# A hybrid mLSTM and short-conv block in fp32 on TensorE: post-processing cut into stages that take turns, and a first phase of two interleaved items

## The chip, the cores and the metric

One core of a Trainium2 chip runs the whole program. The metric is the time of one execution on the device in microseconds, as a median over runs. Below, PE is TensorE (its weight loads are PEld), DVE is VectorE, ACT is ScalarE, POOL is GpSimd and SP is SyncE, which here only issues DMAs.

## What is computed

One block over 512 tokens of width 2048, all in fp32:

```python
hn = rmsnorm(h, norm_mix_g)
proj = hn @ w_in + b_in
(q, k, v, o_pre, i_pre, f_pre, cb, cc, ch, gm_pre, gc_pre) = split(proj)
hm = mlstm_chunkwise(q, k, v, i_pre, f_pre)          # 4 heads, dqk 128, dv 256
hm = hm * rsqrt(mean(hm * hm) + EPS) * mlstm_head_g * sigmoid(o_pre)
y_m = hm @ w_branch_m
y_c = (cb * causal_dwconv(cc * ch, conv_w)) @ w_branch_c
h = h + (sigmoid(gm_pre) * y_m + sigmoid(gc_pre) * y_c) @ w_out
hn = rmsnorm(h, norm_ffn_g)
gate, val = split(causal_dwconv(hn @ w_up, ffn_conv_w, ffn_conv_b))   # 5504 each
h = h + (silu(gate) * val) @ w_down
return rmsnorm(h, norm_out_g)
```

## The kernel before

Each large product is done on TensorE in fp32r with operands split in two: a high part (`hi`, a copy on ACT that rounds) and a low part (`lo`, the difference, on DVE), and three matmuls, high by high, high by low, low by high. On top of that the 2 by 2 blocks of a product are formed in seven products instead of eight, which needs sums of weight blocks and of activation blocks. A **weight** (a raw tile, high halves `wh`, low halves `wl`) gets two of its sums by DMA: `fill` puts a block in place from SP's queue (L242, L243) and POOL issues DMAs that add another block to it (L245); DVE makes the other two (`s2` L210, `s4` L215). A **cell** (a pair of activation blocks) has its sums on DVE (`t3` L333, `e` L338, `t4` L343), its high part on ACT (L347), its low part on DVE (L350).

The program is a list of 476 steps (an item, a part q of its contraction), then 16 of another form. A step is 2 cells by 7 products by 3 matmuls of 128 by 256, 42 in all (L271, L272, L273), ahead of which PE waits for the weight's halves and for its banks. The phases in order are x (40 items of 4 steps: the input projection), yc and ym (the branches), out, up (the first feed-forward product), down, and a last part. An item's sums stand in half of bank 3 (`P_BANK`) and in one of two sets of three banks. When the item ends, ACT copies the first part to a z tile (`evac_first`, L295) and DVE makes the rest (`evac_ops`, L301 to L304) in the next step. At the ends of a phase two items are interleaved, their steps in turn.

The order on every engine is written by the loop: in step s DVE makes the two sums of weight s+2, the low parts of weight s+1 and of cells, ACT the high parts of weight s+2. There are six raw tiles, four `wh` and three `wl`, eight activation tiles. Loads are issued by SP, stores by ACT, a step after they are asked for (`late`).

What an item needs after its evacuation is its **post**, a list of pieces with a cost. Before, all pieces stand in one queue, and each step takes pieces from its front as long as a running credit allows. A piece may hold both ACT and DVE work: `normed` (L642, a multiplication by rstd on DVE, 1.22 us) and the activations on ACT behind it are one piece.

Next to it runs a **side** list: of each entry the PE part is issued at the end of a step, the post part at the start of the next one. It uses bank 7 (`SIDE`). The row sums, the gates and, from step 38, the four mLSTM heads go through it (24 entries a head): `b_pe` and `b_post` form the decayed scores, `v_pe` and `v_post` transpose v, `c_pe` and `c_post` form the output rows and their normalisation (L600 to L613), `t_pe` and `t_post` transpose back (L621, L627). Between two of them stands an empty entry, `gap`. `rsqrt_cols` (L399 to L411) is a scaling on DVE, a square root on ACT and five DVE operations.

At the start the first item runs alone, steps 0 to 3, one cell at a time as it comes: main matmuls, the gate matmuls of the cell (`gate_mm`, L471 to L476; i and f pre-activations), and the sum over its squares (`sum_tokens`, L420). The raw x of a cell goes through one of five buffers (mA, mB, z2, z0, z1), is scaled into a raw tile (L891, L892), and is squared in place after that (L899); cells 5 to 7 reuse the first three buffers, once their sums are done.

Of the kernel before, what the change touches and what calls it, by code (L numbers as in the profile page):

```python
# [69 lines left out]
def tile_block(ctx: ExitStack, tc: tile.TileContext, xT, w1, w_v0, w_v1, w_v2, w_bm, w_bc, w_out, w_up, w_down,  # L70
# [126 lines left out]
    def weight_task(it, q):  # L197
# [35 lines left out]
        t.load, t.sums, t.hi, t.lo = load, [s2, s4], hi, lo  # L233
        return t
# [20 lines left out]
    def rows_load(w, c0):  # L255
        def load(raw, q):
# [50 lines left out]
    def cell_task(xs, c, d, scale=None, key=None, eight=False):  # L307
# [14 lines left out]

        def diff():
# [3 lines left out]
        def t3():  # L327
            x = slots(t.raw)
            if scale:
                for ap, k in zip(two_k(), (k1, k2)):  # L330
                    A.activation(ap, ap, AF.Copy, scale=scale(k))
# [24 lines left out]
        t.two, m = two_k, 6 * SW if eight else NW  # L356
        t.cost = (0.65, 1.7) if eight else (1.35, 1.95)
# [3 lines left out]
    def direct_cell(xs, c, it, d=None, scale=None, key=None, eight=False):  # L361
# [11 lines left out]
        def t3():  # L373
            assert it.done
            a, b = t.two()
            if d is not None:
                V.tensor_add(a, a, it.z[:, :T])
                V.scalar_tensor_tensor(b, it.z[:, T:], -1.0, b, op0=ALU.mult, op1=ALU.subtract)
            else:
                A.activation(a, it.z[:, :T], AF.Copy, scale=scale(k1))  # L380
                A.activation(b, it.z[:, T:], AF.Copy, scale=scale(k2))
# [17 lines left out]
    def rsqrt_cols(dst, src, scale, eps, n):  # L399

        v, y, t = sm("nv")[:, :n], sm("ny")[:, :n], sm("nt")[:, :n]
# [21 lines left out]
    def rows_stages(ps, dst, diag, nt=4):  # L423

        def cols_post():
            rsqrt_cols(rs1[:, :nt], ps[:, :nt], 1.0 / D, EPS, nt)
# [33 lines left out]
    def gate_mm(c, x):  # L460
# [918 lines left out]
```

## Time and profile before

| what | value |
|---|---|
| median of 3 runs | 2686.89 us (2686.54 to 2688.54) |
| profiled execution, its own time | 2686.18 us |
| its span | 2684.5 us |
| busy, PE / DVE / ACT / POOL | 96% / 79% / 48% / 30% |
| granted PE clock, mean | 0.99 |

The span is the part of the execution in which the engines have instructions; the own time is measured around it, 1.7 us more. A row of the profile that reads "out<-in" names the tiles by their names in the program without their numbers, and "L273" is line 273 of the kernel. A wait is put down to the one that ended last.

### The profile page before, as it was taken

Reading aid. Unit: us, or ns where it says so; the run is one execution under the profiler, and the core shown is the slowest. Engines: PE = TensorE matmul, PEld = TensorE weight load, DVE = VectorE, ACT = ScalarE, POOL = GpSimd, SP = SyncE. Lnnn points to the kernel's source line nnn. Section 1 sums busy time; section 2 is a strip of 40 time slices with the busy share of each in tenths; the row PEclk is TensorE's granted clock in tenths of the full one; section 3 lists DMA queues with packets and bytes.
Section 4 is the critical chain, followed back from the end, with each engine's and each line's share of the span. In section 5 each row is a group of like instructions: output and inputs, shape, how many; then the busy total and the mean of one; then the engine's idle time right before and its main releaser. Section 6 shows DMA issues by size and latency. Waiting matters only on the chain.

```text
span 2684.5 us, 55468 instructions
## 1 busy us (share of the span) xinstructions
PE 2587.5 (96%) x21148; PEld 2564.8 (96%) x21148; DVE 2112.7 (79%) x3304; ACT 1278.2 (48%) x1735; POOL 801.6 (30%) x931
## 2 busy tenths in 40 slices
PE   7899999999999999999799999999999999999998
PEld 6899998999999999899799999999999989999997
DVE  5677777887777788977889988888888887676756
ACT  6444554445554443444545444444444554444433
POOL 3343333233333211121233333333333223232320
PEclk9899999999999999999999999999999999999999
DMA  7799989898989797797788888889888889798976
GB/s 193 177 230 235 246 228 229 215 243 223 253 228 233 205 297 221 212 252 207 204 223 219 223 222 225 221 222 228 218 222 227 206 216 226 188 226 207 238 173 200
DMA packets 464860, 594.64 MB, mean 222 GB/s; under 512 B 43040, under 2 KB 299040, under 8 KB 464592
## 3 DMA queue, kind: packets, MB, share of 16 engines
q1 hardware_dynamic: 303120, 420.84, 49.5%
q0 software_dynamic: 134240, 125.09, 31.6%
q10 hardware_dynamic: 27232, 45.17, 4.6%
q8 instruction: 165, 2.70, 0.4%
q14 instruction: 103, 0.84, 0.1%
HBM read 533.26 MB, written 57.67 MB: 220 GB/s over the span
## 4 chain that ended last, share of the span: by engine, by line
PE 52%; DVE 6%; DMA 4%; issue 2%; ACT 1%; POOL 0%; SPq 0%; DVEq 0%; POOLq 0%; ACTq 0%
PE bank L273 17%; PE bank L271 17%; PE bank L272 17%; DMA raw<-in_w_down_dram 2%; DVE wl L229 2%; DVE act L350 1%; DMA raw<-in_w_out_dram 1%; DMA raw<-in_w_up_dram 1%; DVE z L302 1%; DVE z L301 0%; PE bank L420 0%; PE bank L1095 0%; PE bank L1096 0%; DVE raw L210 0%; PE bank L1097 0%
## 5 line engine op out<-in xcount | busy, mean ns | idle before, releaser
L273 PE MATMUL bank<-act,wl 128*128 128x256 f32 x6760 | 1924.0, 285 | 39.3 <-DVE wl L229 35.9
L271 PE MATMUL bank<-act,wh 128*128 128x256 f32 x6760 | 1930.9, 286 | 14.7 <-DVE z L301 8.1
L272 PE MATMUL bank<-act,wh 128*128 128x256 f32 x6760 | 1919.7, 284 | 0.3 <-DVE act L350 0.3
L273 PEld LDWEIGHTS bank<-act,wl 128*128 128x128 f32 x6760 | 1304.2, 193 | 47.2 <-DVE wl L229 42.9
L271 PEld LDWEIGHTS bank<-act,wh 128*128 128x128 f32 x6760 | 1304.4, 193 | 19.3 <-DVE z L301 9.1
L272 PEld LDWEIGHTS bank<-act,wh 128*128 128x128 f32 x6760 | 1304.2, 193 | 3.6 <-issue 1.8
L225 ACT ACTIVATE wh<-raw 128x896 fp32r<-128x896 f32 x856 | 804.0, 951 | 1018.5 <-PE bank L272 682.0
L229 DVE TENSOR_TENSOR wl<-raw,wh 128x896 fp32r<-128x896 f32 x856 | 928.5, 1086 | 220.2 <-PE bank L273 149.6
L245 POOL DMA_DIRECT2D raw<-in_w_up_dram x344 | 299.1, 957 | 616.6 <-DMA raw<-in_w_up_dram 252.1
L245 POOL DMA_DIRECT2D raw<-in_w_dram x288 | 251.2, 950 | 551.2 <-DMA raw<-in_w_dram 274.3
L210 DVE TENSOR_TENSOR raw<-raw 128x256 f32<-128x256 f32 x428 | 179.2, 419 | 40.6 <-DMA raw<-in_w_down_dram 21.6
L245 POOL DMA_DIRECT2D raw<-in_w_down_dram x112 | 100.4, 1017 | 279.8 <-DMA raw<-in_w_down_dram 126.4
L215 DVE TENSOR_TENSOR raw<-raw 128x256 f32<-128x256 f32 x428 | 178.5, 417 | 0.2
L347 ACT ACTIVATE act<-xraw 128x1792 fp32r<-128x1792 f32 (+1 forms) x52 | 85.6, 1646 | 67.3 <-DVE xraw L343 56.6
L301 DVE TENSOR_TENSOR z<-bank,z 128x512 f32<-128x512 f32 x131 | 89.9, 686 | 28.4 <-ACT z L295 17.2
L183 ACT ACTIVATE wh<-raw 128x256 fp32r<-128x256 f32 x96 | 40.0, 416 | 130.1 <-PE bank L272 117.7
L350 DVE TENSOR_TENSOR act<-xraw,act 128x1792 fp32r<-128x1792 f32 (+1 forms) x52 | 101.7, 1956 | 0.0
L642 DVE TENSOR_TENSOR z<-z,rstd 128x1024 f32<-128x1024 f32 x83 | 101.0, 1218 | 0.0
L302 DVE TENSOR_TENSOR z<-bank,z 128x512 f32<-128x512 f32 x131 | 89.6, 684 | 1.8
L304 DVE TENSOR_TENSOR z<-bank,z 128x512 f32<-128x512 f32 x131 | 89.5, 683 | 0.0
L188 DVE TENSOR_TENSOR wl<-raw,wh 128x256 fp32r<-128x256 f32 x96 | 40.4, 421 | 57.9 <-PE bank L273 33.0
L245 POOL DMA_DIRECT2D raw<-in_w_out_dram x48 | 41.8, 972 | 129.6 <-DMA raw<-in_w_out_dram 64.0
(214 smaller groups left out, 1368.5 us busy)
## 6 DMA issues: line engine op xcount, KB each, us to landing
raw<-in_w_up_dram SPq DMA_DIRECT2D x172, 512.0 KB, 5.8
raw<-in_w_dram SPq DMA_DIRECT2D x144, 512.0 KB, 5.8
raw<-in_w_up_dram SPq DMA_DIRECT2D x344, 128.0 KB, 4.2
raw<-in_w_up_dram POOLq DMA_DIRECT2D x344, 128.0 KB, 5.1
raw<-in_w_down_dram SPq DMA_DIRECT2D x80, 512.0 KB, 5.2
raw<-in_w_dram SPq DMA_DIRECT2D x288, 128.0 KB, 4.1
raw<-in_w_dram POOLq DMA_DIRECT2D x288, 128.0 KB, 5.2
raw<-in_w_out_dram SPq DMA_DIRECT2D x32, 512.0 KB, 5.2
```

The costliest lines, as they stand in the source:

```text
L210: V.tensor_add(x[:, 6], x[:, 5], x[:, 0])
L215: V.tensor_add(x[:, 2], x[:, 6], x[:, 1])
L225: A.activation(seven(t.wh[r]), half(r), AF.Copy)
L229: V.tensor_sub(seven(t.wl[r]), half(r), seven(f(t.wh[r])))
L245: G.dma_start(at(i), a21, accum_op=ALU.add)
L271: PE.matmul(ps, h, xh, start=start, stop=False, skip_group_check=True)
L272: PE.matmul(ps, h, xl, start=False, stop=False, skip_group_check=True)
L273: PE.matmul(ps, l, xh, start=False, stop=stop, skip_group_check=True)
L301: return [lambda: V.tensor_add(z[:, 0:4:3], b0, two(z[:, 1])), lambda: V.tensor_add(z[:, 1:3], b1, two(z[:, 3])), lambda: V.tensor_add(z[: ...
L302: lambda: V.tensor_add(z[:, 1:3], b1, two(z[:, 3])),
L350: V.tensor_sub(t.act[:, NW:NW + m], t.raw[:, :m], f(t.act[:, :m]))
L642: V.tensor_mul(sb_pair(it.z), sb_pair(it.z), two(rstd))
```

## The change

- **Start.** The first two items are interleaved and START = 8 steps are done cell by cell in the order in which cells and weights come. Four weights (`ALONE`: items 0 and 1, q = 0, 1 and 2 of item 0) are loaded bare, without fills and adding DMAs; a new DVE operation `s13` makes those two sums. Cells 5 to 7 are loaded into their own raw tile and squared from there ahead of the scaling. The warm-up tile is cleared first on POOL, with 18 warm-up matmuls and not 20. The gate weights are made in step 8 in a raw slot (`held` takes it out of the loads' count), and `gate_mm` runs in steps 9, 10 and 11. The loads of the small parameters come after the start.
- **Posts.** Every item has its own list; up to two items give one piece each per step. `normed` is a piece of its own, the activations the next, and so for conv, out and up: pieces with DVE work and pieces with ACT work are apart. The order is conv: normed, Identity, product, taps; out: residual, square, sum; up: normed, Identity, taps of the first half, silu with taps of the second, product.
- **Side.** `rsqrt_cols` is cut in two, `rsqrt_a` up to the square root and `rsqrt_b` behind it; the second halves of `b_post` and `c_post` (`b_post2`, `c_post2`) stand in what was the empty entry, so that they run one step later.
- **Cells.** Where a cell is scaled on ACT, the scaling (`t.pre`) is issued a step ahead of its sums when its tile is there.

```diff
+ALONE = ((0, 0), (1, 0), (0, 1), (0, 2))
...
+        def s13():
+
+            x = slots(t.raw)
+            V.tensor_add(x[:, 4:6], x[:, 0:4:3], two(x[:, 2]))
...
         t.load, t.sums, t.hi, t.lo = load, [s2, s4], hi, lo
+        if (it.num, q) in ALONE:
+            t.sums = [s13, s2, s4]
...
-        def load(raw, q, eight=False):
-            if not eight:
+        def load(raw, q, bare=False):
+            if not bare:
                 fill(raw, [w[n, :, k0 + 4 * q + i:k0 + 4 * q + i + 2, :] for n in (n1, n2) for i in (0, 2)])
...
+        t.pre = scaled if scale else None
...
-    def rsqrt_cols(dst, src, scale, eps, n):
+    def rsqrt_a(src, scale, eps, n):
...
         A.activation(y, v, AF.Sqrt)
+
+    def rsqrt_b(dst, n):
...
         V.reciprocal(y, y)
...
     def gate_weights():
-        G.memset(f(gw), 0.0)
+        held[0] = 1
+        gwt = wp.tile([P, NW], F32R, tag="raw", name="gw", bufs=RAW)
...
+        def b_post2(cs):
+            def fn():
...
                 V.scalar_tensor_tensor(p, SIDE[:, :w], QK_SCALE, p, op0=ALU.mult, op1=ALU.mult)
...
-                rsqrt_cols(ff[:, c], ssq[:, c], 1.0 / DV, den[:, c], 1)
+                rsqrt_a(ssq[:, c], 1.0 / DV, den[:, c], 1)
+            return fn
+
+        def c_post2(ct):
+            def fn():
...
+                rsqrt_b(ff[:, c], 1)
                 A.activation(hn, SIDE[:, :DV], AF.Copy, scale=ff[:, c])
...
         for cs in (3, 2, 1, 0):
-            out += [(b_pe(cs), b_post(cs)), gap]
+            out += [(b_pe(cs), b_post(cs)), (noop, b_post2(cs))]
         out += [(v_pe(g), v_post(g)) for g in range(2)] + [gap]
         for ct in range(4):
-            out += [(c_pe(ct), c_post(ct)), gap]
+            out += [(c_pe(ct), c_post(ct)), (noop, c_post2(ct))]
         return out + [(t_pe(b), t_post(b)) for b in range(2)]
...
             def fn():
-                normed(it)
                 A.activation(a, a, AF.Identity, bias=bias(C_Q + h))
                 A.activation(b, b, AF.Identity, bias=bias(C_K + h), scale=-1.0)
                 store(qk_d[h], it.z, ("qk", h))
-            return [(1.2, fn)]
+            return [(1.2, lambda: normed(it)), (0, fn)]
...
-            return [(1.2, one), (0.7, two_), (1.4, three), (0.7, four)]
+            return [(1.2, lambda: normed(it)), (0, one), (0.7, two_), (2.1, three)]
...
-            return [(1.3, one), (1.4, two_)]
+            return [(1.3, one), (0, square), (1.4, two_)]
...
-            return [(1.2, one), (1.4, two_), (1.4, three), (0.7, four)]
+            return [(1.2, norm), (0, one), (1.4, two_), (1.4, lambda: (silu(), three())), (0.7, four)]
...
+    START = 8
...
         def load():
+            if c < 5:
+                SP.dma_start(buf[:, :T], xT[k1])
+                SP.dma_start(buf[:, T:2 * T], xT[k2])
+            else:
+                cell_load()
...
         def t3():
...
+            if c < 5:
+                t.new_raw()
+                srcs = buf[:, :T], buf[:, T:2 * T]
+            else:
+                srcs = t.two()
+                square(srcs)
...
-    phase(x_items, X, [x_task(c) for c in range(8)], first_pair=False)
+    phase(x_items, X, [x_task(c) for c in range(8)])
...
+    for _ in range(18):
+        PE.matmul(bank[6], warm[:, :P], warm, start=True, stop=True)
...
+    todo_mm = deque((s, r) for s in range(START) for r in range(2))
     start_sums(order[0])
-    cells = 0
-    for i in range(n_start):
+    for i in range(at[START]):
         start_sums(order[i + 1])
...
-            cell_mm(steps[q][0], q, r, wt[q])
-            gate_mm(cells, X[cells])
-            sum_tokens(SIDE, sqs.pop(cells), 2, 4, cells == 0, cells == 7)
...
+            cell_mm(it, q, r, wt[s])
+            if s % 2 == 0:
+                sum_tokens(SIDE, sqs.pop(c), 2, 4, c == 0, c == 7)
+            if q == 3 and r == 1:
+                evac_first(it)
...
+    cols_a()
+    cols_b()
+    side.append((rows_pe, rows_post))
+
+    def gate_step(s):
+
+        if s == START:
+            gate_weights()
+        elif s < START + 4:
+            for c in range(3 * (s - START - 1), min(8, 3 * (s - START))):
+                gate_mm(c, X[c])
+            if s == START + 3:
+                A.activation(gb[4], GATE, AF.Copy, scale=mrow)
+                held[0] = 0
...
+                side.append((noop, scaled))
+                side.extend(gate_stages())
...
             for r in range(2):
                 cell_mm(it, q, r, wt[s])
             wt[s] = None
+            if s < START + 4:
+                gate_step(s)
...
-            while posts and (credit > posts[0][0] / 2 or any(x[2] in urgent for x in posts) or not main):
-                cost, fn, _ = posts.popleft()
+            rush = not main or any(x[0] in urgent for x in posts)
+            for x in list(posts)[:2]:
+                cost, fn = x[1][0]
+                if not rush and cost and credit <= cost / 2:
+                    break
+                x[1].popleft()
                 credit -= cost
                 fn()
...
+        for t in cells_at.get(s + 3, []):
+            if t.pre and t.raw is not None and (not t.after_end or t.after_end.done):
+                t.pre()
+                t.pre = None
```

On DVE, at the program's start, the rows before are (xraw is a cell, act its split form, raw a weight):

```order
L333 TENSOR_TENSOR xraw_168<-xraw_168 128x512
L338 SCALAR_TENSOR_TENSOR xraw_168<-xraw_168 128x256
L343 SCALAR_TENSOR_TENSOR xraw_168<-xraw_168 128x256
L210 TENSOR_TENSOR raw_112<-raw_112 128x256
L215 TENSOR_TENSOR raw_112<-raw_112 128x256
L350 TENSOR_TENSOR act_174<-xraw_168,act_174 128x1792
L456 TENSOR_TENSOR gw<-mC,gw 128x32 x4
L333 TENSOR_TENSOR xraw_203<-xraw_203 128x512
L338 SCALAR_TENSOR_TENSOR xraw_203<-xraw_203 128x256
L343 SCALAR_TENSOR_TENSOR xraw_203<-xraw_203 128x256
L229 TENSOR_TENSOR wl_212<-raw_112,wh_179 128x896
L229 TENSOR_TENSOR wl_214<-raw_112,wh_181 128x896
```

and in the changed kernel

```order
L342 TENSOR_TENSOR xraw_156<-xraw_156 128x512
L347 SCALAR_TENSOR_TENSOR xraw_156<-xraw_156 128x256
L352 SCALAR_TENSOR_TENSOR xraw_156<-xraw_156 128x256
L211 TENSOR_TENSOR raw_145<-raw_145 128x512
L216 TENSOR_TENSOR raw_145<-raw_145 128x256
L221 TENSOR_TENSOR raw_145<-raw_145 128x256
L359 TENSOR_TENSOR act_162<-xraw_156,act_162 128x1792
L342 TENSOR_TENSOR xraw_175<-xraw_175 128x512
L347 SCALAR_TENSOR_TENSOR xraw_175<-xraw_175 128x256
L352 SCALAR_TENSOR_TENSOR xraw_175<-xraw_175 128x256
L235 TENSOR_TENSOR wl_184<-raw_145,wh_168 128x896
L235 TENSOR_TENSOR wl_186<-raw_145,wh_170 128x896
```

The gate weights' low parts (L456) are gone from here, and row L211 is the new `s13` of the first weight.

On ACT, at the end of the gates, before (mB and mC are gate rows, z_92 is z0 with q and k of the first item, z_93 is z1; L147 is the store, L295 the next item's first evacuation):

```order
L225 ACTIVATE wh_924<-raw_604 128x896 [waits PE_49]
L653 ACTIVATE z_92<-z_92,pcol 128x512 [waits DVE_49]
L654 ACTIVATE z_92<-z_92,pcol 128x512
L225 ACTIVATE wh_939<-raw_658 128x896 [waits DMASW5_49,DMASW4_49,DMAHW7_49,DVE_49,PE_49]
L512 ACT_TABLE_LOAD [waits DVE_49]
L512 ACTIVATE mB<-mB 128x512 [waits Pool_49]
L147 DMA qk_d<-z_92 128x1024 [waits DMAHW7_49,Activation_49]
L295 ACTIVATE z_93<-bank_83 128x256 [waits PE_49]
```

and after (L148 is the store, L303 the first evacuation, L1258 reads the gate bank)

```order
L231 ACTIVATE wh_1118<-raw_754 128x896 [waits DMASW2_49,DMASW3_49,DVE_49,DMAHW3_49,PE_49,Activation_49]
L1258 ACTIVATE mC<-bank_86,mrow 128x512 [waits PE_49]
L690 ACTIVATE z_92<-z_92,pcol 128x512 [waits DMASW4_49]
L691 ACTIVATE z_92<-z_92,pcol 128x512
L148 DMA qk_d<-z_92 128x1024 [waits DMAHW6_49,Activation_49]
L303 ACTIVATE z_92<-bank_83 128x256 [waits DMAHW6_49]
L231 ACTIVATE wh_1193<-raw_754 128x896
```

Before, the evacuation that follows the store of z0 writes z1; after, it writes z0 itself, and it waits for the store's queue (DMAHW6).

On PE, at the end of a step within the first head, before (L600 is `c_pe`, bank_87 is SIDE):

```order
L272 MATMUL bank_83<-act_209,wh_3927 128x256
L273 MATMUL bank_83<-act_209,wl_3941 128x256
L600 MATMUL bank_87<-mB,mA 128x258 x3
L271 MATMUL bank_80<-act_269,wh_3939 128x256
L272 MATMUL bank_80<-act_269,wh_3939 128x256
L273 MATMUL bank_80<-act_269,wl_4014 128x256 [waits DVE_49]
```

and after (L631 is `c_pe`)

```order
L280 MATMUL bank_83<-act_181,wh_3915 128x256
L281 MATMUL bank_83<-act_181,wl_3929 128x256
L631 MATMUL bank_87<-mB,mA 128x258 [waits Activation_49]
L631 MATMUL bank_87<-mB,mA 128x258 x2
L279 MATMUL bank_80<-act_268,wh_3927 128x256
L280 MATMUL bank_80<-act_268,wh_3927 128x256
L281 MATMUL bank_80<-act_268,wl_3996 128x256 [waits DVE_49]
```

`c_pe` now waits for ACT ahead of its first matmul here. On ACT the same stretch reads, before (L606 to L613 are `c_post`)

```order
L225 ACTIVATE wh_3807<-raw_3542 128x896 [waits DMASW1_49,DMASW0_49,DMAHW0_49,DVE_49,PE_49]
L606 ACTIVATE den<-bank_87 128x1
L608 ACTIVATE z_91,ssq<-bank_87 128x256
L406 ACT_TABLE_LOAD
L406 ACTIVATE ny<-nv 128x1 [waits DVE_49]
L613 ACTIVATE z_91<-bank_87,ff 128x256 [waits DVE_49,Activation_49]
L147 DMA cb_d<-z_92 128x2x512 [waits DMAHW1_49]
L225 ACTIVATE wh_3867<-raw_3542 128x896 [waits PE_49]
```

and after (L637 to L422 are `c_post`, L651 is in `c_post2`)

```order
L637 ACTIVATE den<-bank_87 128x1
L639 ACTIVATE z_91,ssq<-bank_87 128x256
L422 ACT_TABLE_LOAD
L422 ACTIVATE ny<-nv 128x1 [waits DVE_49]
L231 ACTIVATE wh_3846<-raw_3527 128x896 [waits PE_49,Activation_49]
L758 ACTIVATE z_92<-z_92,pcol 128x512
L759 ACTIVATE z_92<-z_92,pcol 128x512
L231 ACTIVATE wh_3860<-raw_3592 128x896 [waits DMASW2_49,DMASW3_49,DVE_49,DMAHW3_49,PE_49,Activation_49]
L651 ACTIVATE z_91<-bank_87,ff 128x256 [waits DVE_49,Activation_49]
```

The copy out of SIDE by ff, L613 before, stood right behind the square root; as L651 it stands behind two wh copies and two other activations of the next step.

More of the change, by code (lines that the diff above doesn't have):

```diff
@@ L255, in rows_load, with load @@
     def rows_load(w, c0):
-        def load(raw, q):
+        def load(raw, q, bare=False):
             fill(raw, [w[:, 4 * q + i:4 * q + i + 2, c0 + b * P:c0 + (b + 1) * P] for b in range(2) for i in (0, 2)])
@@ L375, in t3, with scaled @@
             a, b = t.two()
[L376 to L381, printed above, removed]
+            V.tensor_add(a, a, it.z[:, :T])
+            V.scalar_tensor_tensor(b, it.z[:, T:], -1.0, b, op0=ALU.mult, op1=ALU.subtract)
             it.z_read = True
             cell_t3()
-        it.z_read = False
-        t.load, t.sums = load, [t3] + t.sums[1:]
+        def scaled():
+            assert it.done
+            for ap, z, k in zip(t.two(), (it.z[:, :T], it.z[:, T:]), (k1, k2)):
+                A.activation(ap, z, AF.Copy, scale=scale(k))
+            it.z_read = True
+        it.z_read = False
+        t.load = load
+        if d is not None:
+            t.sums = [t3] + t.sums[1:]
+        else:
+            t.pre = scaled
         t.cost = (t.cost[0] + (1.35 if d is not None else 0), t.cost[1])
@@ L879, in x_task, with square @@
         t = cell_task(X, c, xT)
-        cell_t3 = t.sums[0]
+        cell_t3, cell_load = t.sums[0], t.load
         buf = xbufs[c % 5]
         def load():
+            if c < 5:
[3 more added lines that the diff above has]
+                cell_load()
+        def square(srcs):
             assert c < 5 or c - 5 not in sqs
             sqs[c] = buf
-            SP.dma_start(buf[:, :T], xT[k1])
-            SP.dma_start(buf[:, T:2 * T], xT[k2])
+            for i, src in enumerate(srcs):
+                w = src.shape[-1]
+                A.activation(buf[:, i * w:(i + 1) * w], src, AF.Square)
         def t3():
-            t.new_raw()
-            A.activation(t.raw[:, 5 * SW:], buf[:, :T], AF.Copy, scale=g_mix(k1))
-            A.activation(t.raw[:, :2 * SW], buf[:, T:2 * T], AF.Copy, scale=g_mix(k2))
+            if c < 5:
+                t.new_raw()
+                srcs = buf[:, :T], buf[:, T:2 * T]
+            else:
+                srcs = t.two()
+                square(srcs)
+            for ap, src, k in zip(t.two(), srcs, (k1, k2)):
+                A.activation(ap, src, AF.Copy, scale=g_mix(k))
             cell_t3()
@@ L1004, in tile_block @@
         if n < 8:
[L1005 removed]
+            k = t.cell
         else:
@@ L1115, in last_scale @@
                      h.rearrange("p (j t) -> p j t", j=2))
-    loads()
+    warm = actp.tile([P, T], F32R, tag="act", name="warm")
+    G.memset(f(warm), 0.0)
+    for _ in range(18):
+        PE.matmul(bank[6], warm[:, :P], warm, start=True, stop=True)
+    del warm
     A.dma_start(pcol[:, :16], par[:, :16])
-    A.dma_start(gst, w_v0[:, :, DV:DV + 8])
-    G.memset(f(gw), 0.0)
     G.memset(ones, 1.0)
@@ L1128, in tile_block @@
         G.memset(mrow[32 * h:32 * h + 2], 1.0)
-    warm = actp.tile([P, T], F32R, tag="act", name="warm")
-    G.memset(f(warm), 0.0)
-    for _ in range(20):
-        PE.matmul(bank[6], warm[:, :P], warm, start=True, stop=True)
-    del warm
+    loads()
+    A.dma_start(gst, w_v0[:, :, DV:DV + 8])
     def small_loads():
@@ L1201, in tile_block @@
     finals, lq, lsum = deque(), [], []
-    for s in range(4, len(steps)):
+    for s in range(START, len(steps)):
         it, q = steps[s]
@@ L1219, in tile_block @@
             evs += evac_ops(i)
-            for cost, fn in i.post(i):
-                posts.append((cost, fn, i.num))
+            posts.append((i.num, deque(i.post(i))))
         ended = []
```

143 lines of the change are left out of this document (78 added, 65 removed).

## Prediction

> **What bounds the kernel now.** I read the page's first lines, then a table of windows, to see where TensorE (PE) is the limit and where it waits. A window's columns are its length, busy us of PE, PEld, DVE, ACT and POOL (with instructions), the granted PE clock, the DMA share and GB/s.
>
> ```profile
> PE 2587.5 (96%) x21148; PEld 2564.8 (96%) x21148; DVE 2112.7 (79%) x3304; ACT 1278.2 (48%) x1735; POOL 801.6 (30%) x931
> ```
>
> ```profile
> 26.40:77.40 51.00, 50.61 (x393) 48.92 (x392) 35.27 (x44) 34.74 (x38) 12.36 (x15) 0.97 0.69 173
> 77.40:133.65 56.25, 47.77 (x353) 45.91 (x352) 41.49 (x80) 25.56 (x33) 16.71 (x19) 0.88 0.74 174
> 275.00:410.00 135.00, 134.82 (x1100) 133.23 (x1099) 100.59 (x177) 71.02 (x108) 46.01 (x57) 1.00 0.91 236
> 410.00:670.00 260.00, 249.86 (x2017) 245.29 (x2017) 202.76 (x356) 131.33 (x203) 82.22 (x102) 1.00 0.89 227
> 133.65:159.48 25.83, 25.83 (x219) 25.83 (x218) 19.81 (x31) 11.04 (x13) 10.93 (x10) 1.00 1.03 221
> 1276.00:1336.00 60.00, 45.87 (x331) 43.49 (x330) 49.80 (x78) 32.79 (x39) 14.82 (x17) 0.91 0.73 191
> 1380.00:1480.00 100.00, 96.61 (x799) 95.80 (x799) 91.23 (x134) 49.41 (x61) 31.32 (x36) 1.00 0.85 211
> 1500.00:1600.00 100.00, 100.00 (x836) 100.00 (x835) 87.76 (x130) 48.02 (x60) 34.76 (x40) 1.00 0.88 222
> ```
>
> In 1500 to 1600 PE never idles: 836 matmuls of 256 columns in 100 us are 0.1196 us each, 5.02 us for a step of 42. Such stretches fill most of the span, and since the change takes no main matmul away, they can't get shorter. What can move lies in islands: the start (steps 0 to 12, up to 133.65), the mLSTM heads (the 275 row loses 0.2 us, the 410 row 10.1), the passage from out to up (14.1 of 60 idle), and the early up items (3.4 of 100). The waits name what ends last there. First PE at 100 to 118, then 400 to 670, 1276 to 1336, 1380 to 1480 and 2218 to 2236 (total, times, longest):
>
> ```profile
> PE bank L271 <- ACT z L295: 3.8, 1, 3.8
> PE bank L273 <- DVE wl L229: 3.7, 1, 3.7
> ```
>
> ```profile
> PE bank L273 <- DVE wl L229: 3.9, 3, 1.7
> PE bank L584 <- ACT mB L593: 3.4, 2, 1.7
> PE bank L621 <- DVE mB L627: 2.0, 2, 1.8
> ```
>
> ```profile
> PE bank L273 <- DVE wl L229: 6.6, 4, 2.1
> PE bank L271 <- DVE z L301: 4.0, 2, 3.2
> PE bank L431 <- DVE mC L428: 3.3, 1, 3.3
> ```
>
> ```profile
> PE bank L273 <- DVE wl L229: 3.4, 4, 1.3
> ```
>
> ```profile
> PE bank L271 <- ACT z L295: 2.5, 1, 2.5
> ```
>
> L273 waits for wl, the low half of a weight, which DVE makes one step ahead. DVE is in order, so whatever DVE waited for a little earlier is what PE pays for. DVE's own waits at 1276 to 1336, 400 to 620 and 1380 to 1480:
>
> ```profile
> DVE xraw L333 <- ACT xraw L381: 3.9, 3, 1.3
> DVE xraw L333 <- ACT xraw L331: 1.9, 1, 1.9
> DVE mC L769 <- ACT mB L764: 1.6, 1, 1.6
> DVE mC L769 <- ACT mA L764: 1.2, 1, 1.2
> DVE raw L210 <- DMA raw<-in_w_up_dram: 0.9, 1, 0.9
> ```
>
> ```profile
> DVE mA L577 <- POOL mA L575: 17.8, 8, 4.8
> DVE z L692 <- ACT z L689: 8.7, 8, 1.8
> ```
>
> ```profile
> DVE mB L793 <- ACT mB L789: 3.7, 2, 1.9
> DVE mA L793 <- ACT mA L789: 3.1, 2, 1.6
> ```
>
> All of these but the DMA row are cases in which ACT or POOL makes something and DVE wants it at once, in one stage. The change pulls such pairs a step apart.
>
> **The start.** These are group rows of 26 to 78 (count, busy us, mean ns), and timeline rows of the gate chain and of PE's step 12.
>
> ```profile
> L350 DVE TENSOR_TENSOR act<-xraw,act 128x1792 fp32r<-128x1792 f32 x7 | 14.1, 2018 | 0.0
> L347 ACT ACTIVATE act<-xraw 128x1792 fp32r<-128x1792 f32 x7 | 11.9, 1700 | 12.2 <-DVE xraw L343 12.2
> L229 DVE TENSOR_TENSOR wl<-raw,wh 128x896 fp32r<-128x896 f32 x10 | 10.4, 1084 | 0.0
> L225 ACT ACTIVATE wh<-raw 128x896 fp32r<-128x896 f32 x10 | 9.1, 946 | 2.9 <-PE bank L272 1.7 <-PE bank L476 0.9
> L899 ACT ACTIVATE z<-z 128x1024 f32<-128x1024 f32 x4 | 4.2, 1042 | 0.0
> L333 DVE TENSOR_TENSOR xraw<-xraw 128x512 f32<-128x512 f32 x6 | 4.2, 694 | 9.7 <-ACT xraw L892 9.7
> L338 DVE SCALAR_TENSOR_TENSOR xraw<-xraw 128x256 f32<-128x256 f32 x6 | 2.5, 425 | 0.2
> L891 ACT ACTIVATE xraw<-z,pcol 128x512 f32<-128x512 f32 x4 | 2.8, 710 | 0.1
> ```
>
> ```profile
> 94.61 0.48 DVE L487 TENSOR_SCALAR mA<-mC,bic 128x512 f32<-128x512 f32 x1
> ...
> 102.40 1.22 DVE L642 TENSOR_TENSOR z<-z,rstd 128x1024 f32<-128x1024 f32 x1
> ```
>
> ```profile
> 133.65 0.36 PE L271 MATMUL bank<-act,wh 128*128 128x256 f32 x1
> ```
>
> ```profile
> qk_d<-z ACTq DMA_DIRECT2D x4, 512.0 KB, 4.2
> ```
>
> Before, PE needs 51 us for four steps: 20.1 of main work, the rest gate matmuls and sums of squares. A cell's gate is 3 matmuls of 512 columns and 9 of 256, 15 × 0.1196 = 1.8 us, eight cells 14.4; the sums are then at most 51 − 20.1 − 14.4 = 16.5, some 15 without the small waits.
>
> After, eight steps run before the steady loop. PE has 8 × 5.02 + 15 = 55 us of work there, but DVE and ACT hand over one weight and one cell in turn, each waiting for the other: wh 2 × 0.95 (0.1 of it overlapped), two scalings 1.3, the cell's sums 0.69 + 2 × 0.43, the low part of the cell 2.0, and, with a bare load, s13 at 0.69 (as L333, same shape) and s2 and s4 at 0.43 each. That is about 8.2 us for a pair with a bare load and 7.5 with a filled one, and 1.2 more for cells 5 to 7, whose two squares now stand ahead of the scaling. I take the first wl at 16.3 (no accumulating DMA is waited for; the first main matmul of before came at 26.4). Eight pairs then end at 16 + 4 × 8.2 + 4 × 7.5 + 3 × 1.2 less the last low part, hence step 7's end at 81 to 83. There follow a table load, the square root and its columns ahead of the next wl, which puts step 9 at about 90. The gates go into steps 9 to 11: 3 × 5.02 + 14.4 = 29.5, so step 12 begins at 120 where before it began at 133.65: **−13.5**.
>
> It is given back. At the end of step 11 ACT reads the gate bank (0.7, as L891 with the same 512 columns), biases q and k of item 0 (2 × 0.71), stores z0 to qk_d, and then has the first evacuation of item 2, into z0, which must wait for that store to land: 4.2. All in all that evacuation ends 0.7 + 1.4 + 0.1 + 4.2 + 0.4 = 6.8 us after step 12 began; PE wants its bank 2.5 us in, so PE waits 4.3, as it did in the L295 row above. DVE starts from there, 7 us late, on the stretch with most for it to do: five steps at 2.7 (two sums of 0.43, two wl of 1.08, less overlap), three evacuations at 2.3, the gate chain 7.8 (94.61 to 102.40, with ACT's tables inside), two scalings by rstd at 1.22, 0.7 for the gates, and about 3 of conv pieces and negated columns: 34, so step 17 comes at X + 39 to 41 (X is step 12's start) where PE alone would need 25.1. Before, the same chain lay in steps 5 to 8, was paid there, and the five steps from 133.65 cost 25.8 (their row in the table, PE busy throughout). Loss 14. **Start in all: 0**, between −8 (the chain half hidden) and +5 (the gaps all add up).
>
> The Trainium skill ("TensorE: Matmul & The Clock Gate", Part 1) says that an idle window of some 3.4 us halves PE's clock until a busy window has passed. This trace agrees in kind (0.88 granted in 77.4 to 133.65, around two waits of 3.7). By it each further gap of that length costs 1.7 us as an estimate, and the start of after may have three: the total would be 2689 instead of 2684.
>
> **The heads.** Their per-head stages lose DVE waits of 17.8 and 8.7 us (L577 after POOL's select, L692), which were behind three wl stalls (3.9), two L584 stalls behind ACT (3.4) and an L621 one of 1.8: −9. In exchange c_post2 (five small DVE operations and an ACT copy out of SIDE) runs in the very step at whose end PE wants to write SIDE for the next c_pe or t_pe. Nothing of before shows that pair, since a whole empty step lay between. The nearest row is L621 behind L627, also a same-step use of SIDE: 0.2 in one case, 1.8 in the other of those two waits. I take 0.4 where DVE has its full lead, 1.1 after an evacuation and 3.3 once per head that overlaps conv pieces: three heads at 3, the second at 7.4, 16.4, and 0.9 for the same pairing at b_post2. Net **+8**; bounds −5 (20 gates at 0.2, less 9) and +20 (16 at 1.8, less 9). The value lies in the middle, nearer the worse row because DVE is 78% busy there (202.8 of 260).
>
> **Out to up.** The waits on L331 and L381 (5.8) go because the scaling is issued a step earlier, the two on L764 (2.8) because the square has its own stage. 14.1 us idle; the DMA wait stays, the row sum at L431 stays because its square root only moves two steps back, and evacuations pay the rest. Of 8.6 I take −6.4. Bounds −12 (with the clock, 0.91) and −3.
>
> **Early up.** Four wl stalls, 3.4 in all, come behind the four waits at L793 for ACT's first stage, a step apart from now on: −4.4 with the small idles next to them (100 − 96.6 is 3.4; the clock and missing records leave up to 5). I keep **−4**, bounds −3 and −5. Later up items have no stall to lose.
>
> **Down's start.** Item pieces are flushed there in one go in both kernels, now with silu between two DVE pieces and ACT's evacuation behind a store: +1.5 on the 2.5 of L271; bounds 0 and +4.
>
> Bare loads take 8 accumulating DMAs off POOL and 8 fills off SP in the first 50 us; the clearing of the warm-up tile goes first on POOL. Both are inside the start's 16.3. The x loads of cells 5 to 7 take raw slots in SP's queue, which lies ahead there by the DMA share of 0.69. `held` takes one raw slot for four steps: cover is the ring of six, and without it one load comes a step late, 1 us at most.
>
> **Sum:** 0 + 8 − 6.4 − 4 + 1.5 − 1 (small ends) = −2. The profiled execution's own time is 2686.2 and the median 2686.9, 0.7 above: 2684.2 to 2684.9. I say 2684.5.
>
> **Rivals.**
> Start kept: no store is waited for at step 12, or DVE has slack enough for the chain, as the row of 77.4 to 133.65 leaves 14.8 us of DVE idle. Then of −13.5 some −10 stay: 2675. Against it: DVE's idle time there is mostly waiting for ACT, and the store stands in ACT's order right ahead of the evacuation.
> Heads' gates: 16 same-step uses of SIDE at the 1.8 of the worse L621 instead of 1.0 in the mean. +20 in place of +8: 2696.5, slower. It decides from 1.55 us a gate on. For it: after the change ACT's copy also queues behind a wh of 0.95. Against it: the better L621 shows 0.2.
> Nothing moves: steady PE sets the end, DVE's late stretches only change places (the chain and flushes remain), 2687.
> Clock: the new gaps halve PE's clock. A granted 0.88 over 56.25 us is 6.8 us of clock taken; part fell on idle time, and if two thirds of it recur on top of my sum, 2689. For it: the gap at step 12 is longer than either of before's. Against it: in 1276 to 1336, with 14.1 us idle, 0.91 was granted and 5.4 us of clock went, most of it in the idle time. The rule of the clock gate cited above is this case.
>
> **Chances.** A measurement here tells from no change what is over 0.2%, 5.4 us. The forecast 0.40 (own range 2679 to 2690), start kept 0.25, heads' gates 0.18, nothing 0.09, clock 0.08. Faster takes 0.25 and 0.06 of the forecast's lower end; slower takes 0.18, 0.02 of the clock and 0.02 of the forecast. The range goes from 2670 (start kept, and out to up at its −12 end) to 2697 (heads at +20, the rest as summed): about 0.1 left out on each side.
>
> **What would show it.** First main matmul near 12 and step 12 near 120; a PE wait of about 4 for ACT's first evacuation shortly after; step 17 within 3 us of before's 159.5. In the heads PE waits of c_pe for ACT's z, summing to 16, and no L577 or L692 kind of DVE wait above 1 us. No wl waits at 1380 to 1480. I am wrong if step 17 comes more than 6 us earlier, or if the heads' gates sum to under 5 or over 25.

## The result: slower, 1.0049 of the time before

The changed kernel takes 2699.3 us as a median of 5 runs (2698.0 to 2700.7) against 2686.9; the ratio is 1.0049 with an interval of 1.0038 to 1.0060. The forecast was 2684.5 within 2670 to 2697, the likeliest case "no change"; the kernel is about half a percent slower instead, and its time lies outside that range. The profiled execution has a span of 2697.7, 13.2 more than before.

First the page's busy line of the changed kernel, then its windows over the stages (columns as in the prediction), then two windows of before over the same steps as the fourth and the fifth.

```profile
PE 2594.2 (96%) x21146; PEld 2569.8 (95%) x21146; DVE 2114.0 (78%) x3308; ACT 1283.2 (48%) x1741; POOL 799.7 (30%) x922
```

```profile
11.76:86.35 74.59, 58.46 (x464) 57.09 (x465) 55.05 (x81) 46.69 (x54) 21.18 (x26) 0.93 0.79 204
86.35:122.97 36.62, 36.62 (x267) 34.85 (x268) 17.86 (x29) 9.48 (x20) 9.79 (x13) 0.96 0.40 85
122.97:163.59 40.62, 31.19 (x219) 29.84 (x217) 25.79 (x47) 20.04 (x26) 12.46 (x14) 0.87 0.75 172
262.11:896.89 634.78, 615.00 (x4966) 605.25 (x4965) 471.27 (x800) 322.83 (x473) 210.27 (x250) 0.99 0.90 228
1305.06:1357.78 52.72, 45.05 (x349) 43.21 (x348) 50.92 (x80) 31.58 (x38) 18.25 (x21) 0.97 0.90 237
1394.00:1494.00 100.00, 100.00 (x836) 100.00 (x835) 94.16 (x139) 51.96 (x66) 34.14 (x40) 1.00 0.89 225
```

```profile
255.10:875.49 620.39, 609.89 (x4966) 602.13 (x4965) 468.86 (x800) 320.03 (x472) 203.71 (x248) 1.00 0.91 233
1283.80:1344.90 61.10, 47.80 (x346) 45.62 (x347) 53.54 (x84) 31.72 (x37) 18.07 (x22) 0.92 0.75 198
```

The matmuls are the same in number; what moved is idle time, and PE's busy time, which is 6.7 longer. Step 12 begins at 122.97 (133.65 before), yet the five steps from there take 40.6 instead of 25.7. The steps with the heads (36 to 150) take 14.4 longer. The passage to up takes 8.4 less, and the early up items run at 836 matmuls in 100 us, with no gap left.

Steps can be found in each trace by counting main matmuls (42 a step, 48 in a few). The table gives the microseconds between the starts of the steps named, for all kernels of this study; "from 0" is the time at which step 36 begins. Each is one execution, the one profiled. The kernels are made in the sections below.

| kernel | from 0 to 36 | 12 to 36 | 36 to 160 | 160 to 224 | 224 to 260 | 260 to 395 | 395 to 428 | span |
|---|---|---|---|---|---|---|---|---|
| before | 255.1 | 121.4 | 670.8 | 357.9 | 206.6 | 681.4 | 186.8 | 2684.5 |
| changed | 262.1 | 139.1 | 685.2 | 357.8 | 193.8 | 680.4 | 191.8 | 2697.7 |
| store_early (a repeat of it) | 263.7 | 138.6 | 683.3 | 357.5 | 193.1 | 680.4 | 186.9 | 2690.8 |
| c_one | 269.2 | 138.9 | 665.8 | 356.8 | 192.9 | 680.4 | 187.7 | 2678.9 |
| head_gap | 264.9 | 138.9 | 662.8 | 356.4 | 193.6 | 680.4 | 189.5 | 2674.0 |
| old_start | 256.4 | 121.5 | 687.5 | 359.3 | 194.0 | 680.4 | 188.8 | 2694.6 |
| gap_old | 256.5 | 121.5 | 667.1 | 357.5 | 194.2 | 680.4 | 187.9 | 2670.1 |
| store2 | 255.4 | 131.6 | 684.0 | 357.0 | 193.8 | 680.4 | 188.6 | 2689.8 |
| cols_late | 267.2 | 138.6 | 685.8 | 357.6 | 192.9 | 680.4 | 191.6 | 2702.9 |
| gap_fix | 255.0 | 131.8 | 661.7 | 359.0 | 194.1 | 680.4 | 186.7 | 2662.8 |
| gap_store | 256.6 | 131.7 | 660.8 | 357.4 | 193.0 | 680.4 | 191.7 | 2666.7 |
| rush | 261.6 | 131.6 | 663.6 | 358.6 | 193.1 | 680.4 | 183.5 | 2668.0 |
| late_scale | 256.5 | 131.6 | 660.4 | 359.5 | 197.9 | 680.4 | 191.0 | 2672.5 |
| norm_two | 256.6 | 131.7 | 661.9 | 357.0 | 204.9 | 704.2 | 194.0 | 2704.3 |

So after minus before is 7.0 at the start, 14.4 in the x phase with the heads, −12.8 from 224 to 260, 5.0 where down begins. The 5.0 is not a property of the program: its repeat has 0.1 there. Nor are single microseconds in the first column: the changed kernel, its repeat, `c_one` and `head_gap` have the same first 36 steps and reach step 36 at 262.1 to 269.2. From step 12 on the four agree within 0.5, so the start is best read in the second column.

PE's waits in the changed kernel, first in 112 to 172, then in 262 to 897; last, PE's waits of before over the same steps as the second:

```profile
PE bank L279 <- ACT z L303: 6.9, 2, 6.4
PE bank L281 <- DVE wl L235: 3.3, 2, 2.6
```

```profile
PE bank L631 <- ACT z L651: 7.5, 5, 2.9
PE bank L659 <- ACT z L651: 7.4, 4, 2.9
PE bank L590 <- DMA mB<-qk_d: 3.8, 2, 2.0
```

```profile
PE bank L273 <- DVE wl L229: 3.9, 3, 1.7
PE bank L584 <- ACT mB L593: 3.4, 2, 1.7
PE bank L621 <- DVE mB L627: 2.3, 4, 1.8
PE bank L565 <- DMA mB<-qk_d: 0.9, 1, 0.9
```

L303 is the evacuation behind the store, L651 ACT's copy out of SIDE in `c_post2`, L631 and L659 the `c_pe` and `t_pe` that wait for it, L590 (L565 before) the first matmul of a head, which needs q and k.

### The profile page after: what moved, and what is told of

Read it like the earlier page. It is cut to its first block, busy times and chain, and to the rows that moved or that the text cites. A ratio compares the mean times of both kernels' runs of the same rounds, so it can differ in the third digit from the quotient of the medians.

```text
span 2697.7 us, 55485 instructions
## 1 busy us (share of the span) xinstructions
PE 2594.2 (96%) x21146; PEld 2569.8 (95%) x21146; DVE 2114.0 (78%) x3308; ACT 1283.2 (48%) x1741; POOL 799.7 (30%) x922
## 4 chain that ended last, share of the span: by engine, by line
PE 56%; DVE 5%; DMA 3%; issue 1%; ACT 0%; POOL 0%; DVEq 0%; SPq 0%; ACTq 0%; POOLq 0%
PE bank L281 18%; PE bank L279 18%; PE bank L280 18%; DVE wl L235 1%; DMA raw<-in_w_down_dram 1%; DVE act L359 1%; DMA raw<-in_w_up_dram 1%; PE bank L1156 0%; PE bank L440 0%; DVE z L310 0%; PE bank L1157 0%; PE bank L1158 0%; DMA raw<-in_w_out_dram 0%; DVE z L309 0%; DMA xraw<-a_d 0%
## 5 line engine op out<-in xcount | busy, mean ns | idle before, releaser
L279 PEld LDWEIGHTS bank<-act,wh 128*128 128x128 f32 x6760 | 1305.5, 193 | 29.1 <-ACT z L303 12.8
L231 ACT ACTIVATE wh<-raw 128x896 fp32r<-128x896 f32 x856 | 812.4, 953 | 1078.1 <-PE bank L280 713.6
L253 POOL DMA_DIRECT2D raw<-in_w_dram x280 | 243.7, 953 | 548.2 <-DMA raw<-in_w_dram 363.4
L309 DVE TENSOR_TENSOR z<-bank,z 128x512 f32<-128x512 f32 x131 | 89.8, 685 | 36.2 <-ACT z L303 26.6
```

The lines of the kernel that those rows point to most:

```text
L231: A.activation(seven(t.wh[r]), half(r), AF.Copy)
L253: G.dma_start(at(i), a21, accum_op=ALU.add)
L279: PE.matmul(ps, h, xh, start=start, stop=False, skip_group_check=True)
L309: return [lambda: V.tensor_add(z[:, 0:4:3], b0, two(z[:, 1])), lambda: V.tensor_add(z[:, 1:3], b1, two(z[:, 3])), lambda: V.tensor_add(z[: ...
```

## The experiments

**The heads.** `c_one` puts the two halves of `c_post` together again; `head_gap` keeps them apart and gives each another empty step. (`both` runs its two arguments in turn.)

```diff
-            out += [(c_pe(ct), c_post(ct)), (noop, c_post2(ct))]
+            out += [(c_pe(ct), both(c_post(ct), c_post2(ct))), gap]      # c_one
+            out += [(c_pe(ct), c_post(ct)), (noop, c_post2(ct)), gap]    # head_gap
```

> The changed kernel with c_post and c_post2 run together again in the step after c_pe, and the empty entry back behind them; b_post2 and all the rest stay as changed. Theory A (PE's write into SIDE at the end of the step waits for ACT's copy out of SIDE in the same step): the four or so waits of 0.3 to 3.1 us per head at c_pe and the first t_pe vanish (14.8 us named in the waits, about 20 with the short ones and the half clock behind the longest); DVE's wait for the square root comes back (some 2 us): the span falls by 14 to 20, to 2678 to 2684. Theory B (the heads are late because DVE is, with the items' pieces now falling elsewhere): the waits only turn into waits for wl, and the span falls by less than 5.

> The changed kernel with c_post2 kept a step behind c_post and an empty entry put behind it, so that a head takes 28 steps and the four end at step 150. Theory A: PE's waits for ACT's copy out of SIDE vanish as in c_one, and DVE doesn't wait for the square root either: span 2676 to 2682, a little below c_one. Theory B: less than 5 us gained, or none.

`c_one` measured 2680.1 (ratio to before 0.9982, 0.9971 to 0.9993), `head_gap` 2674.4 (0.9962, 0.9949 to 0.9974). In the table steps 36 to 160 fall by 19.4 and 22.4 (17.5 and 20.5 against the repeat): theory A. Their spans are 2678.9, as expected, and 2674.0, 2 below what was expected. PE's waits over the steps with the heads, first `c_one`, then `head_gap`:

```profile
PE bank L659 <- DVE mB L665: 2.4, 4, 1.0
PE bank L590 <- DMA mB<-qk_d: 1.4, 2, 0.9
PE bank L281 <- DVE wl L235: 0.4, 1, 0.4
PE bank L279 <- ACT z L303: 0.3, 1, 0.3
```

```profile
PE bank L590 <- DMA mB<-qk_d: 2.2, 1, 2.2
PE bank L659 <- DVE mB L665: 0.6, 1, 0.6
```

The nine waits for L651 are gone, and waits for wl haven't come in their place (0.4 in `c_one`, none in `head_gap`). `c_one` pays with DVE waits for the square root, of which little reaches PE:

```profile
DVE ny L427 <- ACT ny L422: 10.0, 16, 1.1
```

**The start.** `store_early` was meant to bring the first store forward:

```diff
-    hold = 2
+    hold = 1
...
             if s < START + 4:
+                if s == START + 3:
+                    while dmas:
+                        dmas.pop(0)()
                 gate_step(s)
```

> The changed kernel with the first two items' normed pieces and activations a step earlier, and the store of q and k of the first item issued on ACT ahead of the read of the gate bank. Theory A (the wait of 6.4 us at step 12 for the evacuation, which waits for the store to land, is paid in full): that wait goes, the half clock behind it too: step 17 comes 5 to 8 us earlier, span 2690 to 2693. Theory B (the gate chain on DVE sets when step 17 comes, whatever PE waits for at step 12): other waits take its place, step 17 moves by less than 2, span 2696 to 2698.

It decided nothing: the credit still held the pieces back, so that every engine got the changed kernel's instructions in the changed kernel's order. It serves as a repeat: 2694.1, ratio 1.0039 (1.0024 to 1.0054), and its span, 2690.8, shows that one profile of this program may lie 7 us from another. `store2` adds what was missing.

```diff
-            rush = not main or any(x[0] in urgent for x in posts)
+            rush = not main or s < START + 4 or any(x[0] in urgent for x in posts)
```

> The changed kernel with the first two items' normed pieces and activations forced a step earlier, and both q and k stores issued on ACT ahead of the read of the gate bank, so that the first is on its way some 6 us before step 12. Theory A (the wait of 6 us for the evacuation at step 12 is paid in full): it goes, with the half clock behind it, and step 12 to step 17 shrink from 40 us to 32 to 34. Theory B (the gate chain on DVE sets when step 17 comes): waits for wl or for the next evacuation take its place and the stretch shrinks by under 2.5 us.

ACT in the changed kernel shows what was to go: the store's issue and the evacuation that waits for its landing.

```profile
125.10 0.35 ACTq L148 DMA_DIRECT2D qk_d<-z  x1
131.24 0.38 ACT L303 ACTIVATE z<-bank 128x256 f32<-128x256 f32 x1 [6.17 <-DMA qk_d<-z]
```

In `store2` steps 12 to 17 and PE's waits from 112 to 172 read

```profile
123.77:156.84 33.07, 28.72 (x218) 27.61 (x217) 25.64 (x47) 17.61 (x22) 13.60 (x14) 0.95 0.85 185
```

```profile
PE bank L281 <- DVE wl L235: 3.3, 2, 2.6
PE bank L508 <- DVE mC L1263: 1.3, 1, 1.3
PE bank L279 <- ACT z L303: 0.4, 1, 0.4
PE bank L554 <- DVE ccol L558: 0.4, 1, 0.4
```

40.6 became 33.1, theory A, and step 36 begins at 255.4, 0.3 from before's. Ratio 1.0016 (1.0007 to 1.0026), 2691.8. In these profiles the store's wait is the start's whole loss against before. Without it, the 9.9 us by which step 12 comes earlier in `store2` are spent on 33.1 + 17.8 = 50.9 us for steps 12 to 20. Before, these steps took 40.8, since most of the gate chain was done ahead of them. (`store2`'s wl waits are the changed kernel's.)

What sets the five steps shows on DVE. These are the two L309 in them, each the beginning of an item's evacuation on DVE, in the changed kernel and then in `store2`:

```profile
131.66 0.69 DVE L309 TENSOR_TENSOR z<-bank,z 128x512 f32<-128x512 f32 x1 [13.04 <-ACT z L303]
161.65 0.69 DVE L309 TENSOR_TENSOR z<-bank,z 128x512 f32<-128x512 f32 x1
```

```profile
124.96 0.69 DVE L309 TENSOR_TENSOR z<-bank,z 128x512 f32<-128x512 f32 x1 [5.53 <-ACT z L303]
154.91 0.68 DVE L309 TENSOR_TENSOR z<-bank,z 128x512 f32<-128x512 f32 x1
```

From one to the other it is 30.0 us in both. The chain begins 8.7 us after step 12 in the one and 1.2 in the other, and that difference, 7.5, is what the steps differ by. PE's clock in them, 0.87 and 0.95 granted, changes nothing on top, since PE waits for this chain.

`cols_late` goes after PE's wait at the start of step 8, which reads in the changed kernel

```profile
PE bank L279 <- DVE z L309: 5.5, 1, 5.5
```

> The changed kernel with the second half of the row's square root (cols_b) put behind the two items' evacuation on DVE in step 8 and not ahead of it. PE's wait of 5.5 us at the start of step 8 holds DVE's own wait of 3.7 us for the square root on ACT: theory A, step 8 to step 9 come 3 to 4 us earlier, and so does step 12. Theory B (the weights' chain sets step 9 anyway): step 8 starts earlier, step 9 and 12 by under 1 us.

```diff
-    cols_b()
+    side_posts.append(cols_b)
```

It measured 2704.2, ratio 1.0043 (1.0021 to 1.0065). PE's wait at step 8 moves to L454, which needs what `cols_b` makes (85 to 100):

```profile
PE bank L454 <- DVE z L451: 3.1, 1, 3.1
```

Steps 8 to 12 take 41.5 instead of 36.6. In `cols_late` itself step 8 begins at 87.1 and step 12 at 128.6, no earlier than in the changed kernel. In `gap_fix`, further down, step 8 begins at 81.7, 4.6 earlier, and step 12 at 123.2, so that what is won ahead of step 8 is spent again by step 12: theory B.

> The changed kernel with the start of before (four steps of one item alone, gates and sums cell by cell, filled loads, x through the five buffers); posts, side entries, early scalings and the split square root as changed. If the new start costs 7 us by step 20 as the difference of the two traces says: span 2690 to 2692, with step 17 near 159.5. If the posts' new order costs something there that the old start would suffer too: step 17 at 162 or later, span 2694 or more.

`old_start` measured 2696.7, 1.0047 (1.0032 to 1.0062). Step 17 is at 160.7 and step 36 is 5.7 earlier than in the changed kernel, as the first case had it; but the heads take 2.3 (against the repeat 4.2) longer, and the total is not shorter by more than the profiles differ among themselves. That loss, in the heads above all and then from 160 to 224 and after 428 (1.5 each), is in steps with no edit; why is open.

> head_gap with the start of before. The start of before was 5.7 us ahead by step 36 in the profile of old_start, but the whole run was no shorter. If the start's loss is real and kept: 2667 to 2669. If what is gained at the start is given back later in the x phase: 2672 to 2675.

With the heads cured, `gap_old` has 2672.7, 0.9944 (0.9925 to 0.9962), between the two cases and not told apart from `head_gap` by its interval.

> head_gap with both edits of the start (store2 and cols_late). If both theories A hold, step 17 comes 9 to 12 us earlier than in the changed kernel and the span is 9 to 12 below head_gap's 2674.0: 2662 to 2665. If the chain on DVE sets it: 2671 to 2673.

> head_gap with store2's edit alone, that is gap_fix without cols_late. If cols_late is worth nothing (step 12 came no earlier with it), the span is that of gap_fix, 2662.8, within 3 us. If its 4.6 us at step 8 are kept when the store's wait is gone too, the span is 2666 to 2668.

`gap_fix` (all three edits): 2667.1, **0.9922** (0.9903 to 0.9942). `gap_store` (without `cols_late`): 2671.6, 0.9938 (0.9914 to 0.9963). Both keep the store's gain (131.8 and 131.7 from step 12 to 36). The 3.9 us between the spans are 1.6 by step 36 and 5.0 at 395 to 428, where the repeat differed as much, less 2.7 elsewhere. So what `cols_late` is worth can't be told from this, and it is luck that `gap_fix`'s span, 2662.8, falls where both theories A would have put it.

**Down's start.**

```diff
-            rush = not main or s < START + 4 ...
+            rush = not main or 396 <= s < 404 or s < START + 4 ...
```

> gap_store with the posts of the last two up items taken in the first eight down steps, one piece a step whatever the credit, in place of one flush at the end of those steps. If the flush on ACT and DVE in turn makes PE's wait of 4.6 us for the evacuation at step 404 (after its half clock, 7 us), that wait goes and the span falls by 4 to 6 against gap_store. If DVE, which is behind in those steps anyway (wl waits of 7.7 us in all), only becomes later by the pieces: within 2 us of gap_store.

```profile
2157.00:2237.00 80.00, 71.63 (x574) 70.21 (x573) 72.17 (x108) 38.10 (x53) 22.90 (x26) 0.98 0.89 234
```

for `rush` and, from the same step on, for `gap_store`

```profile
2148.00:2228.00 80.00, 68.00 (x513) 66.58 (x513) 65.42 (x96) 34.00 (x46) 20.18 (x23) 0.91 0.81 209
```

574 matmuls against 513 in 80 us. PE's waits in these windows, `rush` and then `gap_store`:

```profile
PE bank L281 <- DVE wl L235: 7.8, 6, 1.9
PE bank L279 <- DVE z L309: 0.6, 1, 0.6
```

```profile
PE bank L281 <- DVE wl L235: 7.1, 6, 3.0
PE bank L279 <- ACT z L303: 4.9, 1, 4.9
```

The wait for ACT's evacuation at step 404 is gone. Steps 395 to 428 take 183.5, the least of all kernels, 8.2 below `gap_store`. They split at step 404: 395 to 404 takes 58.2 in `rush` and 57.9 in `gap_store`, within what repeats differ by, and 404 to 428 takes 125.3, against 131.0 to 134.4 in all thirteen other profiles. So the flush was the wait, and it costs some 7 us. The totals can't show it: 2668.8 (0.9924, 0.9898 to 0.9950) is not told apart from `gap_store`, and the profiled execution lost 5.1 in its first eight steps, where the program is the same.

**What the changed kernel gained.** `late_scale` takes the early scaling away from `gap_store`, `norm_two` joins ACT's first stage to DVE's taps in up.

```diff
-        for t in cells_at.get(s + 3, []):        # late_scale
-            if t.pre and t.raw is not None and (not t.after_end or t.after_end.done):
-                t.pre()
-                t.pre = None
```

```diff
-            return [(1.2, norm), (0, one), (1.4, two_), ...                  # norm_two
+            return [(1.2, norm), (1.4, lambda: (one(), two_())), ...
```

> gap_store with the cells' scaling on ACT issued with their sums and not a step ahead. Where out passes to up the waits of DVE for the scaling come back (5.8 us in the kernel of before): steps 224 to 228 take 4 to 6 us longer than in gap_store. Rival: the gain there came from the square and the row's square root being apart: less than 1.5 us.

`late_scale` measured 2676.7, 0.9958 (0.9939 to 0.9977). Steps 224 to 228 take 3.5 more, a little under the 4 to 6 expected, and 224 to 260 take 4.9 more; the rival's 1.5 is too little. DVE's waits at 1265 to 1310, `late_scale` and then `gap_store`:

```profile
DVE xraw L342 <- ACT xraw L394: 2.6, 2, 1.3
DVE xraw L342 <- ACT xraw L333: 1.6, 1, 1.6
DVE raw L216 <- DMA raw<-in_w_up_dram: 1.5, 1, 1.5
```

```profile
DVE raw L216 <- DMA raw<-in_w_up_dram: 1.3, 2, 0.9
DVE xraw L342 <- ACT xraw L333: 0.6, 1, 0.6
```

> gap_store with ACT's first stage and DVE's taps of an up item in one piece, so that DVE waits for ACT in the same step, 1.7 us a time. If that coupling was what cost 4.4 us between 1380 and 1480 before: wl waits of PE come back in the early up items, 4 to 6 us in all by step 260, and little after, where DVE's lead is used by nothing else. If DVE's lead of a step covers it: under 1 us.

`norm_two` measured 2706.0, 1.0064 (1.0037 to 1.0091). The coupling costs 11.9 from 224 to 260, nearly all of it from step 240 on, and 23.8 more from 260 to 395, where nothing was expected. The windows of steps 260 to 395, `norm_two` and `gap_store`:

```profile
1480.35:2184.55 704.20, 689.56 (x5672) 682.37 (x5671) 599.37 (x882) 330.01 (x406) 228.54 (x265) 1.00 0.84 213
```

```profile
1467.78:2148.18 680.40, 680.40 (x5673) 680.40 (x5672) 599.56 (x878) 334.19 (x403) 230.13 (x265) 1.00 0.88 221
```

DVE does 599.6 us of work in 680.4 (88%), so it idles 80.8 us, some 2.4 for each of the 34 items. Its waits for ACT's first stage in these steps are, in `norm_two` and then in the kernel of before, where the same stages met:

```profile
DVE mA L836 <- ACT mA L832: 50.9, 17, 3.1
DVE mB L836 <- ACT mB L832: 47.8, 16, 3.0
```

```profile
DVE mB L793 <- ACT mB L789: 29.6, 16, 1.9
DVE mA L793 <- ACT mA L789: 28.9, 16, 1.9
```

Before, the wait was 1.8 an item, which fits into that idle time, and steps 260 to 395 took 681.4, only 1.0 more than now. In `norm_two` it is 3.0, which doesn't fit. So `norm_two` shows what such a wait costs once it is longer than the slack; it is not the coupling of before, whose loss in steps 240 to 260 was 4.4.

## Why the prediction was wrong

The sum failed in two places, the start (forecast 0, measured +7.0) and the heads (forecast +8, measured +14.4), in both by costs that it had at nothing or too small, and not by a wrong chain of waits. Down's start added 3.5, which its repeat does not have.

- **Start, 0 forecast, +7.0.** The mechanism was right: PE waits for ACT's evacuation behind the store, DVE starts late from there, and `store2` takes exactly that away. What failed is the balance of −13.5 and +14. First, "step 12 begins at 120": it began at 123.0. Step 7 ended at 80.9, as summed, and steps 9 to 11 took the 29.5 of the sum. But PE's wait at step 8 was 5.5 where the sum leaves about 3, and behind it step 8 took 7.1 instead of 5.0 at a granted clock of 0.79, a cost that stood among the rivals (clock) and not in the sum. Second, the sum took the steps after 17 at PE's rate. Steps 17 to 20 cost 2.7 more, since the last PE parts of the gate chain (L554, L563) now fall into them. So it is −10.7, +14.9 and +2.7. That the five steps' 40.6 met the forecast's 39 to 41 is in part luck: the store landed 6.1 after its issue and not 4.2, and DVE's chain was some 2 shorter than its sum. Step 17 came 4.1 after before's, outside the 3 given as a sign.
- **Heads, +8 forecast, +14.4.** These are the steps' lengths less those of before, added up by what lies in the steps:

| steps from 36 to 160 | forecast | changed | repeat | `c_one` |
|---|---|---|---|---|
| the 16 at whose end PE wants SIDE (three `c_pe`, the first `t_pe`, per head) | 16.4 | 20.3 | 20.0 | 1.3 |
| 70, 74, 98, where before waited for wl and L584 | | −8.5 | −8.5 | −8.5 |
| 61, 85, 109, 133, with the second `t_pe` (L621 before) | | −0.9 | −1.7 | 0.7 |
| the two rows above together | −9 | −9.4 | −10.3 | −7.8 |
| 65, 89, where L590 needs q and k | 0 | 3.2 | 1.2 | 0.8 |
| all others (the 0.9 is for `b_post2`) | 0.9 | 0.4 | 1.5 | 0.7 |
| sum | 8 | 14.4 | 12.5 | −5.0 |

The stalls removed were priced right. The gates' waits were too: 0.4, 1.1 and 3.3 forecast, 0.15, 1.0 to 1.7 and 2.9 measured, 15.9 in all. What failed is that a gate costs more than its wait: a step with a wait of 0.15 is 0.41 longer, one with 1.70 is 1.96 longer, some 0.25 a gate that the sum had at nothing. The other term at nothing is the load of q and k, for which PE waited 3.8 where it had waited 0.9. The two loads were issued no later in their steps but landed 9.9 and 8.7 us after issue instead of 8.1 and 5.1; the repeat lost less there, and why is open. Step 85 lost its wait of 1.8 and is still 0.2 longer, since behind the wait of 2.9 in step 84 a clock of 0.67 was granted in it.

- **Out to up and early up, −10.4 forecast, −12.8.** Right in sign and size: steps 224 to 228 fell by 7.5 and steps 240 to 260 by 4.4. `late_scale` gives back 3.5 in the former, so that the early scaling is about half of that gain; the rest is not taken apart. For early up the cause is argued from DVE's waits at L793, which are gone, and not shown by an edit that gives just these back. "Later up items have no stall to lose" held (681.4 and 680.4).
- **Down's start, +1.5 forecast, 0 to +5 measured** in two executions of the same program.
- The rival "heads' gates", given 0.18, named the sign and 2696.5, but that this lies near 2699.3 is luck. It was to decide from 1.55 us a gate on, and a gate cost 1.27; the start and down's start made up the rest. Rivals "start kept" and "nothing moves" fell. Of the clock rival, the half clock behind the wait at step 8 was paid (some 2); the 0.87 in 122.97 to 163.59 was not, as `store2` shows.

## What to carry to other kernels

Splitting a post over two steps takes an in-order engine's wait away, but the second half now lies in the step at whose end another engine writes the same buffer: count who wants the buffer next, and give the second half an empty step or leave it whole. Before a tile that is being stored is written again, place a step between the store's issue and the write, and look at what the issue stands behind on its queue: here a read that waits for PE. When a wait recurs in every item, compare it with the engine's idle time per item: at 88% busy and 2.4 us idle an item, a wait of 1.8 cost next to nothing and one of 3.0 cost 23.8 us over 34 items.

## What was not expected of the hardware

The first eight steps of one and the same instruction order took 80.8 in `rush` and 75.7 in `gap_store`, with a lower clock granted:

```profile
11.71:92.55 80.84, 67.41 (x465) 66.34 (x465) 55.03 (x81) 46.79 (x54) 24.90 (x32) 0.80 0.77 192
```

```profile
11.76:87.47 75.71, 62.36 (x465) 61.47 (x465) 54.62 (x81) 46.67 (x54) 22.13 (x28) 0.86 0.78 201
```

The start has idle gaps of 3.2 to 5.5 us, and whether one of them costs the clock differs from one execution to the next. The plainest case is a gap of 3.20 us that ends at 50.03 both in the changed kernel and in `gap_store`, where the order of instructions is still the same. The 10 us behind it read, in the changed kernel and then in `gap_store`:

```profile
50.00:60.00 10.00, 9.97 (x85) 9.98 (x86) 7.62 (x11) 6.53 (x8) 3.22 (x4) 1.00 0.80 196
```

```profile
50.00:60.00 10.00, 9.97 (x51) 9.97 (x52) 7.63 (x11) 6.51 (x8) 3.47 (x4) 0.56 0.80 195
```

The same gap cost nothing in one and 34 matmuls of 85 in the other. The Trainium skill ("TensorE: Matmul & The Clock Gate", Part 1) says that the window over which the gate watches PE runs freely, so that the point at which the clock changes at a kernel's start depends on where in the window the first matmul lands. These rows, 1.00 and 0.56 granted behind one and the same gap, agree with it, though no run here varied the phase by itself.

Next to it, a store of 512 KB landed 6.1 us after its issue at a place where the median of that store was 4.2 before.
